# Forgetting attention in a hybrid decoder layer: the low part of exp made against PSUM, and the row sums split between GpSimd and a column of ones

## The chip, the cores and the metric

The kernel runs on one core of one Trainium2 chip. The metric is the device time of one execution in microseconds (us), lower is better. The engines are TensorE (PE, and PEld for its weight loads), VectorE (DVE), ScalarE (ACT), GpSimd (POOL) and SyncE (SP), which here only issues DMAs. All five run their own instruction streams in order and meet at semaphores.

## The reference

One decoder layer: an RMS norm, one input projection of 2048 x 1024 activations to 5656 columns, three mixers side by side, one output projection, and the residual. All in float32. The mixers are forgetting attention (8 heads of 64), a Mamba-2 scan and a gated linear recurrence. The change touches attention only:

```python
def fox_attention(q, k, v, log_f, q_g, k_g):      # cut
    q = rms_norm(q, q_g); k = rms_norm(k, k_g)
    c = jnp.cumsum(log_f, axis=1)
    # per block of 128 queries, per head:
    logits = einsum(q_i, kt) * scale + (c_i[..., :, None] - ck[:, :, None, :])
    logits = where(kpos <= qpos, logits, -inf)
    p = softmax(logits)
    return einsum(p, vt)
```

## The kernel before

**Two parts of a number.** TensorE's fast float32 form (float32r) rounds its operands. So the kernel splits a float32 tile into a rounded part, called h (high), and the rest, called l (low), and multiplies the parts: h by h, h by l, l by h. A split is usually a copy on ACT into a float32r tile and a subtraction on DVE.

**Stages.** The projections come first (until about 1262 us), and write q, k (high and low), v (`v_d`, per head 128 columns: 64 of each part) and the gate to DRAM. Then comes attention, with pieces of the output projection (the "filler") woven in, until about 2027 us. The rest of the output projection ends the kernel.

**Units and blocks.** A unit is one head and one block of 256 queries (`sb` from 0 to 7); there are 64, most heads in rising order of `sb`. For a unit, the keys are taken 256 at a time. One such step, here called a block and in the code a pair `(j, kp)`, is the element of the schedule; there are 288. The last block of a unit (`kp == sb`) lies on the diagonal and has 384 columns instead of 512.

For one block the steps are these:

- `score(j, kp)`: four matmuls (L974, L975) into a PSUM tile `T` (pool `psT`, three buffers), keys on the partitions, queries in the columns. On the diagonal one more adds the mask (L979). ACT makes e = exp(-T) into an SBUF tile (L982, pool `a4`, four buffers), copies it to `ph`, rounded (L985, pool `a5`, five buffers), and DVE makes `pl = e - ph` (L986). GpSimd adds e to the unit's running sum `acc` (L993, L996). At the unit's last block GpSimd folds that to `w` (L1000, L1001, L1004), ACT rounds it to `ah` (L1007), and GpSimd subtracts for `al` (L1008).
- `av(j, kp)`: four matmuls into the unit's PSUM tile `O` (two buffers), left half: v (128 columns, 64 high, 64 low) by `ph` (L1024) and by `pl` (L1026). Rows 0 to 63 of `O` gather high v, rows 64 to 127 low v.
- `finish(j)`: two matmuls of a matrix of ones `onr` with `ah` and `al` put the row sums of the softmax into the right half of `O` (L1034, L1035). ACT copies the lower half of `O` (L1039), DVE adds the upper half (L1040), GpSimd multiplies by the gate (L1041). The result and the sums go to DRAM (L1044, L1046); the division comes later, in the output projection.

**Maxima.** Before a unit's scores the row maxima are needed. `maxima(j)` makes them from its own matmuls (L932, PSUM tile `S`, two buffers) and DVE reductions (L937, L940, L942), in steps spread over the blocks of the unit before. Its first step also issues loads on SP: q for the next pair of units (`load_q`, L804 and two more), the gate, and once per head the next head's k and v (`load_head`). `flip(j)` turns the maxima into a row: a transpose on PE (L956) and two copies on ACT (L957, L958) into row 96 of the tile `q3`, which the score matmuls read. There are two `q3` buffers, one for each pair of units.

**Order.** A loop over the blocks calls, in turn, `score` of block i, the flip and the maxima steps that fall on i, `av` of block i - 3 (`AVL = 3`), `finish` of a unit whose last `av` was one block before, and a share of filler. The tile framework's scheduler then orders each engine's stream by a timing model of its own, with the program's order as the priority, and it adds the semaphores and gives out buffers.

Of the kernel before, what the change touches and what calls it, by code (L numbers as in the profile page):

```python
# [8 lines left out]
F32 = mybir.dt.float32  # L9
F32R = mybir.dt.float32r  # L10
# [8 lines left out]
P = 128  # L19
# [17 lines left out]
HP = 700  # L37
AHEAD = 1
AVL = 3
NDV = 3  # L40
UP, DOWN = (0, 1, 2, 3, 4, 5, 6, 7), (7, 6, 5, 4, 3, 2, 1, 0)
ORD = (DOWN,) + (UP,) * 6 + (DOWN,)
# [5 lines left out]
def hybrid_block(ctx, tc, x, norm_g, w_in, q_norm_g, k_norm_g, forget_b, ssd_conv_w, ssd_conv_b,  # L48
# [314 lines left out]
    def group_v(vpool, g):  # L363
        cols = [(C_V + g * 256, 256)]
        if g == 0:
            cols += [(C_F, 8), (C_DT, 16)]
        w = weights(cols)
        for t2 in range(8):
            if g == 0:
                pss = [proj_tok(w, t2 * 2 + i, f"pv{g}_{t2 * 2 + i}") for i in range(2)]  # L370
            else:
                ps = proj_tok2(w, t2, f"pv{g}_{t2}")
                pss = [ps[:, i, :] for i in range(2)]
            for i, ps in enumerate(pss):
                t = t2 * 2 + i
                vs = vpool.tile([P, 4, P], F32R, name=f"vs{g}_{t}", tag="qk")
                pv = ps[:, 0:256].rearrange("p (h d) -> p h d", d=64)
                A.activation(vs[:, :, 0:64], pv, AF.Copy, scale=0.5)
                V.scalar_tensor_tensor(vs[:, :, 64:128], pv, 0.5, vs[:, :, 0:64].bitcast(F32),
                                       op0=ALU.mult, op1=ALU.subtract)  # L380
                if g == 0:
                    V.tensor_copy(etot[:, t, 0:8], ps[:, 256:264])
                    V.tensor_copy(dt[:, t, :], ps[:, 264:280])
                dma(v_d[t * P:(t + 1) * P, g * 4:g * 4 + 4, :], vs.bitcast(F32))
# [345 lines left out]
    for c in range(NT):  # L730
        for g in range(2):
            nxt = ssd_unit(c, g)
            if store is not None:
# [11 lines left out]
    cx = ExitStack()  # L745
    kc = cx.enter_context(tpool(name="kc", bufs=1, side="right"))
    kvA = cx.enter_context(tpool(name="kvA", bufs=1, side="right"))
    kq = cx.enter_context(tpool(name="kq", bufs=2, side="right"))
    units = [(h, sb) for h in range(8) for sb in ORD[h]]

    zm = kc.tile([P, 640], F32, name="zm")
    G.memset(zm, 0.0)
    G.affine_select(out=zm[:, 512:640], in_=zm[:, 512:640], pattern=[[-1, P]],
                    compare_op=ALU.is_ge, fill=-NEG, base=0, channel_multiplier=1)
    onr = kc.tile([P, P], F32R, name="onr")
    V.tensor_copy(onr, ones)
    idr = kc.tile([P, P], F32R, name="idr")
    V.tensor_copy(idr, ident)
    zmt = kc.tile([P, P], F32R, name="zmt")
# [1 line left out]
    mzs = [kc.tile([P, P], F32, name=f"mz{i}") for i in range(2)]  # L761


    q3s = [kc.tile([P, 512], F32R, name=f"q3{i}") for i in range(2)]
    for i in range(2):
        G.memset(mzs[i], 0.0)
    for q3 in q3s:
        G.memset(q3[64:128, :].bitcast(F32), 0.0)
        G.memset(q3[64:66, :].bitcast(F32), 1.0)
    k2s = {}  # L770

    def make_k2(b):
# [9 lines left out]
    def load_head(h):  # L782
        p, b = divmod(h, 2)
        hs = slice(b * 64, b * 64 + 64)
        pool = kvB if b else kvA
        k2 = k2s[b]
        kx = pool.tile([P, S], F32R, name=f"kx{h}", tag="kx")
        vv = pool.tile([P, NT, P], F32R, name=f"vv{h}", tag="vv")
        dma(k2[0:64, :].bitcast(F32), qk_d["k", "h", p][hs, :])
        dma(k2[64:66, :].bitcast(F32), c_d[h].rearrange("i t l -> i (t l)"))  # L790
        dma(kx[0:64, :].bitcast(F32), qk_d["k", "l", p][hs, :])
        dma(kx[64:128, :].bitcast(F32), qk_d["k", "h", p][hs, :])
        dma(vv.bitcast(F32), v_d[:, h, :].rearrange("(t p) c -> p t c", p=P))
        heads[h] = k2, kx, vv

    def load_q(j):
        h, sb = units[j]
        p, b = divmod(h, 2)
        hs = slice(b * 64, b * 64 + 64)
        q3 = q3s[j // 2 % 2]  # L800
        qx = kq.tile([P, 512], F32R, name=f"qx{j}", tag="qx")
        sb -= sb % 2
        qs = slice(sb * 256, sb * 256 + 512)
        dma(q3[0:64, :].bitcast(F32), qk_d["q", "h", p][hs, qs])  # L804
        dma(qx[0:64, :].bitcast(F32), qk_d["q", "h", p][hs, qs])
        dma(qx[64:128, :].bitcast(F32), qk_d["q", "l", p][hs, qs])
        qs_[j // 2] = q3, qx
# [91 lines left out]
    psO = pcx.enter_context(tpool(name="psO", bufs=PB[2], space=PSUM))  # L899
    psP = pcx.enter_context(tpool(name="psP", bufs=PB[3], space=PSUM))  # L900
    make_k2(1)
    U = [{} for _ in units]

    def maxima(j):
# [55 lines left out]
    def score(j, kp):  # L960

        h, sb = units[j]
        u = U[j]
        k2, kx, vv = heads[h]
        q3, qx = qs_[j // 2]
        o = (sb % 2) * 256
        last = kp == sb
        n = 384 if last else 512
        pt = psT.tile([P, 512], F32, name=f"T{j}_{kp}", tag="T")
        for jj in range(2):  # L970
            ks = slice((kp * 2 + jj) * P, (kp * 2 + jj + 1) * P)
            qs = slice(o + P if last and jj else o, o + 256)
            ps = pt[:, 256 * jj:256 * jj + qs.stop - qs.start]
            T.matmul(ps, k2[:, ks], q3[:, qs], start=(jj == 0), stop=False, skip_group_check=True)  # L974
            ins = T.matmul(ps, kx[:, ks], qx[:, qs], start=False, stop=True, skip_group_check=True)  # L975
        if last:

            pv = pt.rearrange("p (a b) -> p a b", b=256)[:, :, 0:P]
            ins = T.matmul(pv, idr, zmt.unsqueeze(1).broadcast_to([P, 2, P]), start=False,  # L979
                           stop=True, skip_group_check=True)  # L980
        e = a4.tile([P, 512], F32, name=f"e{j}_{kp}", tag="e")
        A.activation(e[:, 0:n], pt[:, 0:n], AF.Exp, scale=-1.0)  # L982
        ph = a5.tile([P, 512], F32R, name=f"ph{j}_{kp}", tag="ph")
        pl = a5.tile([P, 512], F32R, name=f"pl{j}_{kp}", tag="pl")
        A.copy(ph[:, 0:n], e[:, 0:n])  # L985
        V.tensor_tensor(pl[:, 0:n], e[:, 0:n], ph[:, 0:n].bitcast(F32), op=ALU.subtract)  # L986
        u[kp] = ph, pl
        if not last:
            if kp == 0:
                u["acc"] = e  # L990
            elif kp == 1:
                acc = a2.tile([P, 512], F32, name=f"ac{j}", tag="ac")
                G.tensor_tensor(acc, u["acc"], e, op=ALU.add)  # L993
                u["acc"] = acc
            else:
                G.tensor_tensor(u["acc"], u["acc"], e, op=ALU.add)  # L996
            return ins
        if sb > 0:
            w = a2.tile([P, 256], F32, name=f"w{j}", tag="w")
            G.tensor_tensor(w, u["acc"][:, 0:256], u["acc"][:, 256:512], op=ALU.add)  # L1000
            G.tensor_tensor(w, w, e[:, 0:256], op=ALU.add)  # L1001
        else:
            w = e
        G.tensor_tensor(w[:, P:256], w[:, P:256], e[:, 256:384], op=ALU.add)  # L1004
        u["ah"] = a2.tile([P, 256], F32R, name=f"ah{j}", tag="ah")
        u["al"] = a2.tile([P, 256], F32R, name=f"al{j}", tag="al")
        A.copy(u["ah"], w[:, 0:256])  # L1007
        G.tensor_tensor(u["al"], w[:, 0:256], u["ah"].bitcast(F32), op=ALU.subtract)  # L1008
        return ins

    def av(j, kp):

        h, sb = units[j]
        u = U[j]
        vv = heads[h][2]
        if kp == 0:
            u["O"] = psO.tile([P, 512], F32, name=f"O{j}", tag="O")
        po = u["O"]
        ph, pl = u.pop(kp)
        for jj in range(2):  # L1020
            kt = kp * 2 + jj
            qs = slice(P if kp == sb and jj else 0, 256)
            cs = slice(256 * jj, 256 * jj + 256 - qs.start)
            T.matmul(po[:, qs], vv[:, kt, :], ph[:, cs], start=(kt == 0), stop=False,  # L1024
                     skip_group_check=True)
            T.matmul(po[:, qs], vv[:, kt, :], pl[:, cs], start=False, stop=(kt == 2 * sb + 1),  # L1026
                     skip_group_check=True)

    def finish(j):
# [1 line left out]
        h, sb = units[j]  # L1031
        u = U[j]
        po = u["O"]
        T.matmul(po[:, 256:512], onr, u["ah"], start=False, stop=False, skip_group_check=True)  # L1034
        T.matmul(po[:, 256:512], onr, u["al"], start=False, stop=True, skip_group_check=True)  # L1035

        tm = a2.tile([64, 512], F32, name=f"tm{j}", tag="tm")
        to = a2.tile([64, 256], F32, name=f"to{j}", tag="to")
        A.copy(tm, po[64:128, :])  # L1039
        V.tensor_tensor(to, po[0:64, 0:256], tm[:, 0:256], op=ALU.add)  # L1040
        G.tensor_tensor(to, to, u["za"], op=ALU.mult)  # L1041
        p, b = divmod(h, 2)
        cs = slice(sb * 256, (sb + 1) * 256)
        dma(at_d[p][b * 64:b * 64 + 64, cs], to)  # L1044
        qt = slice(sb * 2, sb * 2 + 2)
        dma(s_d[qt, h:h + 1, :].rearrange("i o t -> o i t"),  # L1046
            tm[0:1, 256:512].rearrange("o (i t) -> o i t", i=2))
        if h == 7:

            sr = a2.tile([16, P], F32, name=f"sr{j}", tag="sr")  # L1050
# [117 lines left out]
    begin = [tasks.index((j, 0)) for j in range(len(units))]  # L1168
    at = {}
    for j in range(1, len(units)):  # L1170
        a, b = max(0, begin[j - 1] - 1), begin[j] - 1
        st = maxima(j)
        for i, f in enumerate(st):
            at.setdefault(a + i * (b - a) // len(st), []).append(f)
# [52 lines left out]
```

## Time and profile before

| | us |
|---|---|
| median of 3 runs | 2217.47 (2216.0 to 2223.02) |
| the profiled execution | 2201.74 |
| its span, first to last instruction | 2200.0 |
| attention, first score matmul to last `av` | 1262 to 2027 |

| engine | busy over the span, us | share |
|---|---|---|
| PE | 2048.2 | 93% |
| DVE | 1433.3 | 65% |
| ACT | 1019.2 | 46% |
| POOL | 880.2 | 40% |

How to read the rows: a group's row has line, engine, operation, out<-in, shapes and count, then busy us and mean ns of one, then the engine's idle time just before such instructions and what ended it. A row of one line alone has min/median/max in ns and first and last start. A row of waits has the total in us, the number and the longest. A matmul's record covers its passage through the array, so records of neighbouring matmuls overlap and a busy PE is not PE at its peak. The granted clock (PEclk) is TensorE's clock as a share of full speed.

### The profile page before, as it was taken

What the parts mean: (1) busy time and instruction counts of PE and PEld (TensorE: products, weight loads), DVE (VectorE), ACT (ScalarE), POOL (GpSimd) and SP (SyncE); (2) the same over time, 40 slices, a digit from 0 to 9 for tenths busy, and PEclk for the clock granted to TensorE, in tenths of its full rate; (3) what the DMA queues carried; (4) which work ended last, traced back from release to release, by engine and by line L of the source; (5) the groups of instructions that cost most, each with busy time, mean ns of one, the idle gap of its engine ahead of it and who ended that gap; (6) DMA issues with size and microseconds to landing.
All of it is one profiled execution on the core that took longest, in us unless ns stands there. A gap on an engine that the chain in (4) does not pass through costs nothing. (4 is left out here: it accounts for less than half of the span.)

```text
span 2200.0 us, 34666 instructions
## 1 busy us (share of the span) xinstructions
PE 2048.2 (93%) x11941; PEld 1762.5 (80%) x11941; DVE 1433.3 (65%) x2513; ACT 1019.2 (46%) x2113; POOL 880.2 (40%) x898
## 2 busy tenths in 40 slices
PE   7999999999999998999999988888888888988999
PEld 6898888899898987878889777777777776767887
DVE  6657555736456466767654576877787776887333
ACT  7534454525345345444433446555565555554110
POOL 0100000413223145456520167766777776766110
PEclk9999999999999999999999999988999999997999
DMA  5322232121121456677662555252535435232454
GB/s 175 101 76 60 71 104 87 38 61 60 39 74 50 119 161 195 180 213 207 176 185 80 182 146 136 92 137 70 151 109 140 126 93 130 73 111 83 152 169 139
DMA packets 260466, 261.30 MB, mean 119 GB/s; under 512 B 26773, under 2 KB 198833, under 8 KB 258737
## 3 DMA queue, kind: packets, MB, share of 16 engines
q1 hardware_dynamic: 260128, 259.05, 40.3%
q8 instruction: 94, 1.54, 0.3%
q0 software_dynamic: 160, 0.03, 0.1%
q14 instruction: 84, 0.68, 0.1%
HBM read 164.22 MB, written 94.77 MB: 118 GB/s over the span
## 5 line engine op out<-in xcount | busy, mean ns | idle before, releaser
L986 DVE TENSOR_TENSOR pl<-e,ph 128x512 fp32r<-128x512 f32 (+1 forms) x288 | 338.2, 1197 | 46.4 <-ACT ph L985 46.2
L1095 PE MATMUL po<-woh,mh 128*128 128x512 f32 x512 | 208.5, 407 | 5.7 <-DVE xr L1103 3.1
L1026 PE MATMUL O<-pl,vv 128*128 128x256 f32 x576 | 162.9, 313 | 48.8 <-DVE pl L986 47.9
L1096 PE MATMUL po<-wol,mh 128*128 128x512 f32 x512 | 205.6, 401 | 0.0
L1097 PE MATMUL po<-woh,ml 128*128 128x512 f32 x512 | 205.4, 401 | 0.0
L982 ACT ACTIVATE e<-T 128x512 f32<-128x512 f32 (+1 forms) x288 | 162.8, 575 | 85.5 <-PE T L975 48.4
L996 POOL TENSOR_TENSOR ac<-ac,e 128x512 f32<-128x512 f32 x120 | 185.9, 1549 | 23.2 <-ACT e L982 16.1
L1026 PEld LDWEIGHTS O<-pl,vv 128*128 128x128 f32 x576 | 114.8, 199 | 76.3 <-DVE pl L986 73.2
L974 PE MATMUL T<-q,k 128*128 128x256 f32 x576 | 163.2, 305 | 12.9 <-ACT q L958 12.5
L1024 PE MATMUL O<-ph,vv 128*128 128x256 f32 x576 | 154.1, 286 | 15.2 <-ACT ph L985 5.6
L942 DVE TENSOR_REDUCE mc<-S 128x1 f32<-128x512 f32 x192 | 129.9, 682 | 57.8 <-PE S L932 57.6
L985 ACT CAST ph<-e 128x512 fp32r<-128x512 f32 (+1 forms) x288 | 165.3, 597 | 2.8 <-PE O L1024 0.6
L1083 POOL TENSOR_TENSOR ml<-mt,mh 128x512 fp32r<-128x512 f32 x48 | 67.1, 1399 | 244.1 <-ACT mh L1082 244.0
L975 PE MATMUL T<-qx,kx 128*128 128x256 f32 x576 | 156.6, 299 | 0.0
L356 PE MATMUL pxx<-uh,wh 128*128 128x512 f32 x384 | 152.8, 400 | 1.8 <-ACT uh L301 1.7
L357 PE MATMUL pxx<-ul,wh 128*128 128x512 f32 x384 | 153.1, 400 | 0.0
L358 PE MATMUL pxx<-uh,wl 128*128 128x512 f32 x384 | 150.9, 395 | 0.0
L340 PE MATMUL pqk<-wh,uh 128*128 128x256 f32 x512 | 149.4, 292 | 0.0
L344 PE MATMUL pqk<-wh,ul 128*128 128x256 f32 x512 | 149.3, 292 | 0.0
L342 PE MATMUL pqk<-wl,uh 128*128 128x256 f32 x512 | 148.8, 291 | 0.0
L412 DVE SCALAR_TENSOR_TENSOR accx<-rtx,cv,accx 128x512 f32<-128x512 f32 x144 | 108.0, 752 | 57.8 <-ACT accx L409 54.8
L342 PE MATMUL pzs<-wl,uh 128*128 128x256 f32 x512 | 143.5, 281 | 0.0
(351 smaller groups left out, 5925.4 us busy)
## 6 DMA issues: line engine op xcount, KB each, us to landing
ab<-acs_d SPq DMA_DIRECT2D x64, 256.0 KB
pt_d<-xr SPq DMA_DIRECT2D x64, 256.0 KB
wr<-in_w_in_dram SPq DMA_DIRECT2D x112, 128.0 KB
xt<-in_x_dram SPq DMA_DIRECT2D x16, 512.0 KB
xs_d<-stx SPq DMA_DIRECT2D x32, 256.0 KB
v_d<-vs SPq DMA_DIRECT2D x32, 256.0 KB
wr<-in_w_in_dram SPq DMA_DIRECT2D x128, 64.0 KB
zs_d<-zs SPq DMA_DIRECT2D x32, 256.0 KB
```

Of the source, the lines that this page charges most:

```text
L342: T.matmul(ps[:, i, :], h[k][:, sl], wl[k], start=False, stop=False, skip_group_check=True)
L974: T.matmul(ps, k2[:, ks], q3[:, qs], start=(jj == 0), stop=False, skip_group_check=True)
L975: ins = T.matmul(ps, kx[:, ks], qx[:, qs], start=False, stop=True, skip_group_check=True)
L982: A.activation(e[:, 0:n], pt[:, 0:n], AF.Exp, scale=-1.0)
L985: A.copy(ph[:, 0:n], e[:, 0:n])
L986: V.tensor_tensor(pl[:, 0:n], e[:, 0:n], ph[:, 0:n].bitcast(F32), op=ALU.subtract)
L996: G.tensor_tensor(u["acc"], u["acc"], e, op=ALU.add)
L1024: T.matmul(po[:, qs], vv[:, kt, :], ph[:, cs], start=(kt == 0), stop=False, skip_group_check=True)
L1026: T.matmul(po[:, qs], vv[:, kt, :], pl[:, cs], start=False, stop=(kt == 2 * sb + 1), skip_group_check=True)
L1095: T.matmul(ps, mh[:, j, :], h, start=(j == 0), stop=False)
L1096: T.matmul(ps, mh[:, j, :], l, start=False, stop=False)
L1097: T.matmul(ps, ml[:, j, :], h, start=False, stop=(j == 3))
```

## The change

- `score`: no tile e. ACT makes exp(-T) twice, into `ph` (rounded, SBUF) and back into `T` (full, PSUM). DVE makes `pl = T - ph`, one source in PSUM. GpSimd adds `ph` only.
- The order of v's parts is swapped in DRAM (low in 0 to 63, high in 64 to 127), and the SBUF tile `vv` gets two more columns, set to one by GpSimd once per head.
- `av`: the matmul with `pl` takes 65 columns of `vv` (high v and the ones) and adds into the right half of `O`: rows 0 to 63 get high v by `pl`, row 64 the sums of `pl`. The product of low v and `pl` is no longer made.
- `finish`: `onr` has 65 columns, of which only the last is ones, so the sums of `ph` land on row 64 too. ACT makes two copies instead of one, DVE two additions instead of one, with three buffers each.
- Schedule: with `LT = 2` the steps of `maxima` (with their loads) come one block earlier, the flip stays; a third pair of q tiles (`q3`, `qx`), and `qx` moves from a pool of its own to them.

```diff
+LT = 2
...
-                A.activation(vs[:, :, 0:64], pv, AF.Copy, scale=0.5)
-                V.scalar_tensor_tensor(vs[:, :, 64:128], pv, 0.5, vs[:, :, 0:64].bitcast(F32),
+                A.activation(vs[:, :, 64:128], pv, AF.Copy, scale=0.5)
+                V.scalar_tensor_tensor(vs[:, :, 0:64], pv, 0.5, vs[:, :, 64:128].bitcast(F32),
                                        op0=ALU.mult, op1=ALU.subtract)
...
-    onr = kc.tile([P, P], F32R, name="onr")
-    V.tensor_copy(onr, ones)
+    onr = kc.tile([P, 65], F32R, name="onr")
+    G.memset(onr[:, 0:64].bitcast(F32), 0.0)
+    G.memset(onr[:, 64:65].bitcast(F32), 1.0)
...
+    def make_q(pool):
+        i = len(q3s)
+        q3 = pool.tile([P, 512], F32R, name=f"q3{i}")
+        G.memset(q3[64:128, :].bitcast(F32), 0.0)
+        G.memset(q3[64:66, :].bitcast(F32), 1.0)
+        q3s.append(q3)
+        qxs.append(pool.tile([P, 512], F32R, name=f"qx{i}"))
...
-        vv = pool.tile([P, NT, P], F32R, name=f"vv{h}", tag="vv")
+        vv = pool.tile([P, NT, 130], F32R, name=f"vv{h}", tag="vv")
...
-        dma(vv.bitcast(F32), v_d[:, h, :].rearrange("(t p) c -> p t c", p=P))
+        dma(vv[:, :, 0:128].bitcast(F32), v_d[:, h, :].rearrange("(t p) c -> p t c", p=P))
+        G.memset(vv[:, :, 128:130].bitcast(F32), 1.0)
...
-        q3 = q3s[j // 2 % 2]
-        qx = kq.tile([P, 512], F32R, name=f"qx{j}", tag="qx")
+        q3, qx = q3s[j // 2 % 3], qxs[j // 2 % 3]
...
-        e = a4.tile([P, 512], F32, name=f"e{j}_{kp}", tag="e")
-        A.activation(e[:, 0:n], pt[:, 0:n], AF.Exp, scale=-1.0)
         ph = a5.tile([P, 512], F32R, name=f"ph{j}_{kp}", tag="ph")
         pl = a5.tile([P, 512], F32R, name=f"pl{j}_{kp}", tag="pl")
-        A.copy(ph[:, 0:n], e[:, 0:n])
-        V.tensor_tensor(pl[:, 0:n], e[:, 0:n], ph[:, 0:n].bitcast(F32), op=ALU.subtract)
+        A.activation(ph[:, 0:n], pt[:, 0:n], AF.Exp, scale=-1.0)
+        A.activation(pt[:, 0:n], pt[:, 0:n], AF.Exp, scale=-1.0)
+        V.tensor_tensor(pl[:, 0:n], pt[:, 0:n], ph[:, 0:n].bitcast(F32), op=ALU.subtract)
         u[kp] = ph, pl
+        e = ph.bitcast(F32)
...
         else:
-            w = e
+            G.tensor_copy(w, e[:, 0:256])
...
-            T.matmul(po[:, qs], vv[:, kt, :], ph[:, cs], start=(kt == 0), stop=False,
-                     skip_group_check=True)
-            T.matmul(po[:, qs], vv[:, kt, :], pl[:, cs], start=False, stop=(kt == 2 * sb + 1),
+            q2 = slice(256 + qs.start, 512)
+            T.matmul(po[:, qs], vv[:, kt, 0:128], ph[:, cs], start=(kt == 0),
+                     stop=(kt == 2 * sb + 1), skip_group_check=True)
+            T.matmul(po[0:65, q2], vv[:, kt, 64:129], pl[:, cs], start=False, stop=False,
                      skip_group_check=True)
...
-        tm = a2.tile([64, 512], F32, name=f"tm{j}", tag="tm")
-        to = a2.tile([64, 256], F32, name=f"to{j}", tag="to")
-        A.copy(tm, po[64:128, :])
-        V.tensor_tensor(to, po[0:64, 0:256], tm[:, 0:256], op=ALU.add)
+        to = a3.tile([64, 256], F32, name=f"to{j}", tag="to")
+        su = a3.tile([1, 256], F32, name=f"su{j}", tag="su")
+        A.copy(to, po[64:128, 0:256])
+        A.copy(su, po[64:65, 256:512])
+        V.tensor_tensor(to, po[0:64, 0:256], to, op=ALU.add)
+        V.tensor_tensor(to, po[0:64, 256:512], to, op=ALU.add)
...
-        a, b = max(0, begin[j - 1] - 1), begin[j] - 1
+        a, b = max(0, begin[j - 1] - LT), begin[j] - LT
```

More of the change, by code (lines that the diff above doesn't have):

```diff
@@ L747, in hybrid_block @@
     kvA = cx.enter_context(tpool(name="kvA", bufs=1, side="right"))
-    kq = cx.enter_context(tpool(name="kq", bufs=2, side="right"))
     units = [(h, sb) for h in range(8) for sb in ORD[h]]
@@ L761, in hybrid_block @@
     mzs = [kc.tile([P, P], F32, name=f"mz{i}") for i in range(2)]
-    q3s = [kc.tile([P, 512], F32R, name=f"q3{i}") for i in range(2)]
+    q3s, qxs = [], []
+    def make_q(pool):
[5 more added lines that the diff above has]
+        qxs.append(pool.tile([P, 512], F32R, name=f"qx{i}"))
     for i in range(2):
         G.memset(mzs[i], 0.0)
-    for q3 in q3s:
-        G.memset(q3[64:128, :].bitcast(F32), 0.0)
-        G.memset(q3[64:66, :].bitcast(F32), 1.0)
+    for i in range(2):
+        make_q(kc)
     k2s = {}
@@ L901, in hybrid_block @@
     make_k2(1)
+    make_q(a1)
     U = [{} for _ in units]
@@ L997, in score @@
             return ins
+        w = a2.tile([P, 256], F32, name=f"w{j}", tag="w")
         if sb > 0:
-            w = a2.tile([P, 256], F32, name=f"w{j}", tag="w")
             G.tensor_tensor(w, u["acc"][:, 0:256], u["acc"][:, 256:512], op=ALU.add)
@@ L1006, in score @@
         u["al"] = a2.tile([P, 256], F32R, name=f"al{j}", tag="al")
-        A.copy(u["ah"], w[:, 0:256])
-        G.tensor_tensor(u["al"], w[:, 0:256], u["ah"].bitcast(F32), op=ALU.subtract)
+        A.copy(u["ah"], w)
+        G.tensor_tensor(u["al"], w, u["ah"].bitcast(F32), op=ALU.subtract)
         return ins
@@ L1033, in finish @@
         po = u["O"]
-        T.matmul(po[:, 256:512], onr, u["ah"], start=False, stop=False, skip_group_check=True)
-        T.matmul(po[:, 256:512], onr, u["al"], start=False, stop=True, skip_group_check=True)
-        tm = a2.tile([64, 512], F32, name=f"tm{j}", tag="tm")
-        to = a2.tile([64, 256], F32, name=f"to{j}", tag="to")
-        A.copy(tm, po[64:128, :])
-        V.tensor_tensor(to, po[0:64, 0:256], tm[:, 0:256], op=ALU.add)
+        T.matmul(po[0:65, 256:512], onr, u["ah"], start=False, stop=False, skip_group_check=True)
+        T.matmul(po[0:65, 256:512], onr, u["al"], start=False, stop=True, skip_group_check=True)
+        to = a3.tile([64, 256], F32, name=f"to{j}", tag="to")
[4 more added lines that the diff above has]
+        V.tensor_tensor(to, po[0:64, 256:512], to, op=ALU.add)
         G.tensor_tensor(to, to, u["za"], op=ALU.mult)
@@ L1046, in finish @@
         dma(s_d[qt, h:h + 1, :].rearrange("i o t -> o i t"),
-            tm[0:1, 256:512].rearrange("o (i t) -> o i t", i=2))
+            su.rearrange("o (i t) -> o i t", i=2))
         if h == 7:
```

## The prediction

> **What bounds the kernel now.** I read the first lines of the page, then the busy time by window. The attention stage runs from its first score matmul at 1262 us to its last at 2027 us; what follows is output projection alone.
>
> ```profile
> PE 2048.2 (93%) x11941; PEld 1762.5 (80%) x11941; DVE 1433.3 (65%) x2513; ACT 1019.2 (46%) x2113; POOL 880.2 (40%) x898
> ```
>
> ```profile
> core 0: us, PE busy (x) PEld busy (x) DVE busy (x) ACT busy (x) POOL busy (x), PEclk, DMA share, GB/s
> 1262.00:2027.00 765.00, 657.36 (x3671) 554.76 (x3670) 604.36 (x1043) 424.85 (x880) 540.56 (x503) 0.93 0.41 115
> 2027.00:2200.00 173.00, 167.47 (x725) 137.86 (x724) 67.69 (x153) 18.47 (x31) 19.28 (x17) 0.97 0.48 148
> ```
>
> In 765 us, DVE is busy 79%, POOL 71%, ACT 56%. PE's 86% is not its work: the timeline (start, duration) shows how far its records overlap, the groups how many there are.
>
> ```profile
> 1709.23 0.41 PE L975 MATMUL T<-qx,kx 128*128 128x256 f32 x1
> 1709.44 0.41 PE L974 MATMUL T<-q,k 128*128 128x256 f32 x1
> 1711.04 0.39 PE L1096 MATMUL po<-wol,mh 128*128 128x512 f32 x1
> 1711.27 0.39 PE L1097 MATMUL po<-woh,ml 128*128 128x512 f32 x1
> 1711.73 0.28 PE L974 MATMUL T<-q,k 128*128 128x256 f32 x1
> 1711.85 0.28 PE L975 MATMUL T<-qx,kx 128*128 128x256 f32 x1
> ```
>
> ```profile
> L932 PE MATMUL S<-k,q 96*128 96x512 f32 (+3 forms) x311 | 127.2, 415 | 6.0 <-DVE mc L942 2.9 <-DMA q<-qh_d 2.1 <-DVE mz L937 0.2
> L1095 PE MATMUL po<-woh,mh 128*128 128x512 f32 x268 | 111.2, 415 | 4.8 <-DVE xr L1103 3.1 <-DVE xr L1101 0.8
> ```
>
> Starts lie 0.12 us apart for 256 columns and 0.23 for 512 at full clock, 0.21 for 256 at the throttled clock 2 us before. At full clock the stage's matmuls (288 blocks of eight and some 250 at the units' ends with up to 256 columns; 3 x 268 and 311 with up to 512) need 2554 x 0.12 + 1115 x 0.23 = 563 us. So about 200 of the 765 us are waits and slow clock. The next view, waits of PE's weight loads (the loads stand first in line), names them: us in total, times, longest.
>
> ```profile
> PEld O L1026 <- DVE pl L986: 73.2, 99, 3.1
> PEld T L974 <- ACT q L958: 23.7, 35, 1.9
> PEld pm L956 <- DVE mz L940: 14.2, 20, 1.8
> PEld O L1034 <- ACT ah L1007: 10.3, 14, 2.2
> PEld S L932 <- DVE mc L942: 7.8, 18, 1.3
> PEld O L1024 <- DVE to L1040: 5.4, 3, 3.5
> PEld O L1024 <- DVE mz L940: 5.3, 2, 2.6
> PEld O L1035 <- POOL al L1008: 4.5, 11, 1.4
> ```
>
> Most of it ends with DVE, half of that with the subtraction pl = e - ph. The groups of DVE by shape, and two lines outside the busy part of POOL, say why (last rows: min/median/max).
>
> ```profile
> L986 DVE TENSOR_TENSOR pl<-e,ph 128x512 fp32r<-128x512 f32 x224 | 286.5, 1299 | 45.3 <-ACT ph L985 45.1
> L986 DVE TENSOR_TENSOR pl<-e,ph 128x384 fp32r<-128x384 f32 x64 | 53.6, 842 | 1.1 <-ACT ph L985 1.1
> L937 DVE CUSTOM_DVE_ANT_0 jk<-S,zm 128x384 f32<-128x384 f32 x31 | 17.0, 548 | 8.5 <-PE S L932 8.5
> L1040 DVE TENSOR_TENSOR to<-O,tm 64x256 f32<-64x256 f32 x62 | 25.3, 410 | 14.5 <-ACT tm L1039 7.2 <-DMA at_d<-to 6.8
> L1101 DVE SCALAR_TENSOR_TENSOR xr<-po,rsn,xr 128x256 f32<-128x256 f32 x64 | 28.1, 471 | 11.3 <-PE po L1097 11.3
> L1101 DVE SCALAR_TENSOR_TENSOR xo<-po,rsn,xo 128x256 f32<-128x256 f32 x52 | 21.7, 474 | 18.3 <-DMA xo<-pt_d 15.5 <-PE po L1097 2.8
> L1075 DVE TENSOR_TENSOR ml<-mt,mh x16: 683/685/1133, 2018.6 to 2185.3; 128x512 fp32r<-128x512 f32 x16
> L398 DVE SCALAR_TENSOR_TENSOR zt<-th,pza x8: 676/684/689, 1211.4 to 1250.9; 128x512 f32<-128x512 f32 x8
> ```
>
> The same subtraction of two SBUF tiles takes 685 ns (L1075) where POOL is nearly idle, 1299 ns in attention. L1101 reads PSUM and one SBUF tile: 471 ns in attention, 474 mostly in the tail, so POOL does not stretch it. The stretch belongs to two SBUF sources.
>
> **The change part by part.** *pl from PSUM.* One source moves to PSUM. Nearest rows: 684 ns (L398) for 512 columns and 548 (L937) for 384. DVE gives back 224 x (1299 - 684) + 64 x (842 - 548) = 157 us. Ends: 0 if the stretch stays, 157 if it goes; L1101 is nearest in form, so 157. [...]
>
> What does PE get of it? Its 99 waits on pl average 0.74 us; each pl comes 0.6 us sooner, and so do those queued before it, but a faster PE asks sooner. I take three quarters of 73.2: 55 us. Of the 18.5 us behind mc, to and mz, which share DVE's queue, I take half: 9.
>
> *POOL.* The other party gets free too. Means against the shortest:
>
> ```profile
> L996 POOL TENSOR_TENSOR ac<-ac,e x120: 1254/1619/2727, 1265.0 to 2003.7; 128x512 f32<-128x512 f32 x120
> L1001 POOL TENSOR_TENSOR w<-w,e x56: 721/987/1667, 1276.6 to 2020.4; 128x256 f32<-128x256 f32 x56
> L996 POOL TENSOR_TENSOR ac<-ac,e 128x512 f32<-128x512 f32 x120 | 185.9, 1549 | 23.2 <-ACT e L982 16.1 <-PE po L1097 1.2
> L1001 POOL TENSOR_TENSOR w<-w,e 128x256 f32<-128x256 f32 x56 | 53.3, 952 | 3.7 <-ACT e L982 0.2
> L775 POOL MEMSET k<- 1x2048 f32 x1 | 1.8, 1799 | 0.1
> ```
>
> 120 x (1549 - 1254) + 56 x (952 - 721) = 48 us off POOL in these two groups. It adds ph in place of e, at the same time as before. The one path to PE is the end of a unit (ah, al: 14.8 us of waits); a third goes: 5. New on POOL: eight copies for one-block units (at 952 ns, 8 us) and one memset per head behind vv's release. The memset's price is at most L775's 1.8 us; what stands behind it on POOL are the adds of the next units, which PE needs four blocks later. Ends: 0, and 7 heads x 3 blocks x 2.66 us = 56 us of a standing POOL; I put in 1 us a head, 7 lost, since POOL catches up in those four blocks.
>
> *ACT.* The copy to ph becomes the second exponential, PSUM to PSUM.
>
> ```profile
> L985 ACT CAST ph<-e 128x512 fp32r<-128x512 f32 x224 | 134.2, 621 | 1.5 <-PE O L1024 0.4
> L982 ACT ACTIVATE e<-T 128x512 f32<-128x512 f32 x224 | 132.0, 599 | 64.0 <-PE T L975 48.4 <-DVE pl L986 6.3 <-DVE mc L937 1.7
> L1039 ACT COPY tm<-O 64x512 f32<-64x512 f32 x63 | 36.5, 583 | 39.8 <-PE O L1035 21.0 <-DMA s_d<-tm 16.0 <-DVE pl L986 1.8
> ```
>
> 288 x (599 - 621) = -6 us; no row writes PSUM from ACT: it could be dearer or cheaper, and I take 599, the same function from the same tile. In finish, tm's 583 becomes two copies, each of half the columns or fewer and so under 583: between 0 and +37 us. Together at most 31 us on 425, hidden by ACT's 44% idle; without that cover ACT would be at 456 of 663. DVE's second add in finish costs 64 x 410 = 26 us, so DVE's net is 604 - 157 + 26 = 473. The three result buffers in place of two free ACT's 16.0 us behind s_d; nothing of that reaches PE.
>
> *Thinner second matmul, swapped halves of v.* Same count, same 256 columns.
>
> ```profile
> L1026 PEld LDWEIGHTS O<-pl,vv x576: 186/188/338, 1267.7 to 2026.9; 128*128 128x128 f32 x192
> L956 PEld LDWEIGHTS pm<-ident,mz x64: 160/163/284, 1260.5 to 2020.1; 128*97 128x97 f32 x64
> ```
>
> Fewer weight columns load sooner (163 against 188), but matmuls start every 0.12 us, so the loads already overlap. Ends 0 and 576 x 25 ns = 14 us; I take 0. The other vv and vs edits move the same bytes.
>
> *Maxima one block earlier (LT = 2), third q buffer.* A block takes 765 / 288 = 2.66 us. PE's waits for mz and then for q (14.2 + 23.7 = 38) are at most 1.9 us long. One block more of lead covers them, unless the flip's own copies behind two exponentials hold: I take four fifths, 30. The moved steps issue their q, za and head loads on SP one block earlier; the third buffer keeps the q loads from waiting for readers there. I put nothing in for it: little of PE's waiting ends with a DMA.
>
> *Clock.* Granted 0.93 in the stage, 0.97 after it. Fewer gaps should give about 0.95: 0.02 x 563, some 10 us. [...]
>
> *T held longer.* T was free after the first exponential; now after both and pl. Three buffers at 2.66 us allow a stay of 8.0; scores, exponentials and pl need 0.5 + 0.6 + 0.6 + 0.7 = 2.4, and 5.6 remain for DVE's queue. I charge nothing here; it is the main rival.
>
> Sum: 55 + 9 + 5 + 30 + 10 - 7 = 102 us. Attention then takes 663 us, with DVE at 71%, POOL (541 - 48 + 8) at 76%, ACT at most 69%: below DVE's 79% of now. The profiled execution took 2201.7, so 2100 against it; the median is 15.8 above it, hence **2115**.
>
> **The rivals.** *T takes back half.* PE loses its lead: scores of block i+3 wait for pl of block i, where only its second half of av waited. For it: bursts such as this one of DVE are what the lead absorbs; against: three pl shrink from 3.84 to 2.05 us.
>
> ```profile
> 1699.82 3.84 DVE L986 TENSOR_TENSOR pl<-e,ph 128x512 fp32r<-128x512 f32 x3
> ```
>
>  Half of 102 gone: 2166.
>
> *Slower: the T loop decides.* If every block waits for T as long as pl's waiters do now, 288 x 0.74 = 213 us replace 73; less the other 47 of the sum, +93: 2310. It decides from a mean wait of (73 + 47) / 288 = 0.42 us per block. Against: it needs the 5.6 us to be used up regularly.
>
> *Nothing moves.* PE's waits for pl pass to POOL, still over 70% loaded, at each unit's end: 2217.
>
> *DVE was the pace.* Every us off DVE counts, 131, plus LT's 30: 2056. For it: DVE is the fullest engine; against: it idles 161 us.
>
> **How the numbers follow.** Forecast (2065 to 2150) 0.52; half taken back 0.22; nothing 0.06; slower 0.12; below 2065, 0.08. A change within 0.3% (6.7 us) can't be told from none. Faster 0.82, same 0.06, slower 0.12. The range 2060 to 2222 leaves out the slower case and most of the last: 0.19.
>
> **What would show it.** pl at 512 columns near 690 ns (above 900: the stretch was not POOL's doing); the second exponential near 600; DVE's total 1433 down by 130; L996's mean under 1400; waits for pm and q under 10 us; scores waiting for pl under 30 us. If those exceed 120 us, or POOL's memset holds its queue for several us a head, the prediction is wrong.

## The result, and the profile after

The changed kernel takes 2067.61 us (median of 4, 2064.18 to 2072.21) against 2216.73 before: a ratio of 0.9329, interval 0.9294 to 0.9365, or 149 us less. The forecast of faster held, and the time lies in the range (2065 to 2150), 2.6 us from its fast end; the point, 2115, gave 102 of the 149 us. The profiled execution of the kernel before was some 15 us faster than its median, so the profiles show 136.5 us of the difference.

The first lines of the page and the busy time by window, with the attention stage now from 1260 to 1892 us:

```profile
PE 1970.9 (96%) x11941; PEld 1713.8 (83%) x11941; DVE 1303.0 (63%) x2576; ACT 1007.7 (49%) x2177; POOL 803.1 (39%) x918
```

```profile
core 0: us, PE busy (x) PEld busy (x) DVE busy (x) ACT busy (x) POOL busy (x), PEclk, DMA share, GB/s
1260.00:1892.00 632.00, 582.20 (x3674) 506.53 (x3672) 473.63 (x1106) 413.94 (x945) 464.23 (x517) 0.98 0.49 139
1892.00:2063.00 171.00, 165.62 (x725) 136.40 (x723) 70.72 (x157) 18.48 (x31) 19.19 (x17) 0.99 0.49 152
```

Attention shrank from 765 to 632 us, so 133 of the 136.5 us between the two spans (2200.0 and 2063.5) come from there; the projections before it and the tail behind it became about 2 us shorter each. DVE is down from 604 to 474 us, POOL from 541 to 464, ACT from 425 to 414. PE does as many matmuls as before, at a granted clock of 0.98 in place of 0.93.

The waits of PE's weight loads in attention (us in total, times, longest):

```profile
PEld pm L969 <- DVE mz L953: 19.0, 21, 4.0
PEld T L987 <- ACT q L971: 14.4, 24, 2.1
PEld S L945 <- ACT q L971: 7.6, 12, 1.0
...
PEld S L945 <- DVE mc L955: 5.5, 8, 1.8
PEld O L1042 <- DVE pl L998: 5.1, 7, 1.2
PEld O L1050 <- ACT ah L1021: 3.7, 7, 1.3
...
PEld O L1051 <- POOL al L1022: 0.9, 2, 0.7
PEld T L987 <- DVE pl L998: 0.6, 1, 0.6
```

The wait for pl is all but gone: 73.2 us before, 5.1 now, and T waits for pl only 0.6 us. The flip's waits are not gone: 14.2 + 23.7 before, 19.0 + 14.4 now, with 7.6 of S beside them. The groups by shape in that window:

```profile
L998 DVE TENSOR_TENSOR pl<-T,ph 128x512 fp32r<-128x512 f32 x224 | 152.7, 685 | 39.9 <-ACT T L997 37.9 <-PE po L1113 0.3 <-PE S L945 0.3
L998 DVE TENSOR_TENSOR pl<-T,ph 128x384 fp32r<-128x384 f32 x64 | 35.2, 551 | 9.0 <-ACT T L997 8.3
...
L1010 POOL TENSOR_TENSOR ac<-ac,ph 128x512 f32<-128x512 f32 x120 | 156.1, 1301 | 23.1 <-ACT ph L996 17.2 <-DMA xr<-pt_d 1.2
L806 POOL MEMSET vv<- 128x32 f32 x6 | 0.8, 132 | 1.4 <-PE O L1042 1.3
...
L997 ACT ACTIVATE T<-T 128x512 f32<-128x512 f32 x224 | 133.6, 596 | 0.0
```

pl takes 685 ns (1299 before) and GpSimd's addition 1301 (1549): both sides of the old conflict got quicker. The second exponential, PSUM to PSUM, takes 596 ns, the first 597.

### The profile page after: what moved, and what is told of

It reads as the page before. It is cut to its first block, busy times and chain, and to the rows that moved or that the text cites. A ratio compares the mean times of both kernels' runs of the same rounds, so it can differ in the third digit from the quotient of the medians.

```text
span 2063.5 us, 35018 instructions
## 1 busy us (share of the span) xinstructions
PE 1970.9 (96%) x11941; PEld 1713.8 (83%) x11941; DVE 1303.0 (63%) x2576; ACT 1007.7 (49%) x2177; POOL 803.1 (39%) x918
## 4 chain that ended last, share of the span: by engine, by line
PE 41%; DMA 6%; DVE 4%; ACT 4%; issue 2%; POOL 2%; SPq 0%; DVEq 0%; POOLq 0%; ACTq 0%
PE po L1112 5%; PE po L1113 5%; PE po L1114 5%; PE T L987 3%; PE T L988 3%; PE S L945 2%; PE O L1040 2%; PE O L1042 2%; PE py L691 2%; PE pza L358 1%; PE pza L359 1%; PE pza L357 1%; DMA ab<-acs_d 1%; PE pqk L341 1%; PE pqk L343 1%
## 5 line engine op out<-in xcount | busy, mean ns | idle before, releaser
L998 DVE TENSOR_TENSOR pl<-T,ph 128x512 fp32r<-128x512 f32 (+1 forms) x288 | 187.3, 655 | 48.8 <-ACT T L997 46.3
L996 ACT ACTIVATE ph<-T 128x512 fp32r<-128x512 f32 (+1 forms) x288 | 165.1, 573 | 88.7 <-PE T L988 60.5
L1010 POOL TENSOR_TENSOR ac<-ac,ph 128x512 f32<-128x512 f32 x120 | 156.1, 1301 | 23.1 <-ACT ph L996 17.2
L997 ACT ACTIVATE T<-T 128x512 f32<-128x512 f32 (+1 forms) x288 | 164.9, 572 | 0.0
L987 PE MATMUL T<-q,k 128*128 128x256 f32 x576 | 150.0, 287 | 9.6 <-ACT q L971 6.8
L1040 PE MATMUL O<-ph,vv 128*128 128x256 f32 x576 | 149.0, 280 | 0.9 <-ACT ph L996 0.4
L1042 PE MATMUL O<-pl,vv 128*65 128x256 f32 x576 | 142.2, 279 | 3.4 <-DVE pl L998 2.8
L988 PE MATMUL T<-qx,kx 128*128 128x256 f32 x576 | 143.7, 283 | 0.0
L345 PE MATMUL pzs<-wh,ul 128*128 128x256 f32 x512 | 143.4, 280 | 0.0
L341 PE MATMUL pzs<-wh,uh 128*128 128x256 f32 x512 | 143.0, 281 | 0.0
```

Of the source, the lines that this page charges most:

```text
L341: T.matmul(ps[:, i, :], h[k][:, sl], wh[k], start=(k == 0 and i == 0), stop=False, skip_group_check=True)
L345: ins = T.matmul(ps[:, i, :], l[k][:, sl], wh[k], start=False, stop=last, skip_group_check=True)
L998: V.tensor_tensor(pl[:, 0:n], pt[:, 0:n], ph[:, 0:n].bitcast(F32), op=ALU.subtract)
L1040: T.matmul(po[:, qs], vv[:, kt, 0:128], ph[:, cs], start=(kt == 0), stop=(kt == 2 * sb + 1), skip_group_check=True)
L1042: T.matmul(po[0:65, q2], vv[:, kt, 64:129], pl[:, cs], start=False, stop=False, skip_group_check=True)
```

## The experiments

Theory P says that the stretch of pl by GpSimd was the cost. Rival L says that the earlier maxima and the third q buffer bring much of the gain. Each kernel was timed in three rounds beside the kernel before; ratios are to that kernel. Its own median moved between 2213.07 and 2216.73 us from one set of rounds to the next, so between kernels of different sets the ratios are the better measure.

**One part alone: pl from PSUM (x3_psum).**

```diff
 # kernel before (cut)
-        A.activation(e[:, 0:n], pt[:, 0:n], AF.Exp, scale=-1.0)
-        A.copy(ph[:, 0:n], e[:, 0:n])
-        V.tensor_tensor(pl[:, 0:n], e[:, 0:n], ph..., op=ALU.subtract)
+        A.activation(ph[:, 0:n], pt[:, 0:n], AF.Exp, scale=-1.0)
+        A.activation(pt[:, 0:n], pt[:, 0:n], AF.Exp, scale=-1.0)
+        V.tensor_tensor(pl[:, 0:n], pt[:, 0:n], ph..., op=ALU.subtract)
+        e = ph.bitcast(F32)
```

> The kernel before with one part of the change: both exponentials and pl from PSUM, GpSimd adding ph, no tile e. LT, the q buffers, v's layout, the second matmul and finish stay as before (so the sums of pl are left out of the row sums). Theory P (the stretch of pl by GpSimd was the cost, and a source in PSUM takes it away): pl at 512 columns falls from 1299 to about 685 ns and this part alone brings at least 110 of the 149 us, so 2065 to 2105 us. Rival L (the earlier maxima and the third q buffer bring much of it): under 75 us, over 2140. Rival T (the longer stay of T eats part of the gain until LT and the rest give it back): between, with scores waiting for pl over 20 us.

Measured: 2113.46 us, ratio 0.9541 (0.9517 to 0.9564), 102 us less than the 2215.71 beside it. That is two thirds of the gain, a little under what theory P asked for. The time lies in the band of rival T, but not by its cause: scores wait 0.5 us in all for pl at T. pl is at 686 ns and PE's wait for it at 9.2 us. But other waits came up. The window, the group of pl, and waits in the window:

```profile
1268.00:1944.00 676.00, 603.34 (x3672) 528.05 (x3672) 458.81 (x1042) 410.67 (x881) 463.68 (x512) 0.95 0.47 130
```

```profile
L985 DVE TENSOR_TENSOR pl<-T,ph 128x512 fp32r<-128x512 f32 x224 | 153.4, 686 | 41.9 <-ACT T L984 40.7 <-PE po L1096 0.3 <-PE po L1097 0.3
```

```profile
ACT tm L1039 <- DMA s_d<-tm: 35.0, 9, 5.7
...
DVE to L1040 <- DMA at_d<-to: 28.3, 6, 6.1
...
PEld pm L956 <- DVE mz L940: 19.7, 22, 3.6
PEld T L974 <- ACT q L958: 19.3, 37, 0.8
...
PEld O L1034 <- ACT ah L1007: 19.0, 18, 4.2
...
PEld O L1026 <- DVE pl L985: 9.2, 12, 2.6
```

DVE lost 146 us of work there, the stage 89. `finish` now waits longer for its result buffers, whose stores stand in SP's queue: tm 35.0 us (16.0 before) and to 28.3 (6.8 before). PE's wait for ah rose from 10.3 to 19.0 us.

**Then the schedule (x9_psum_lt2).** x3_psum with `LT = 2` and the third pair of q tiles, as in the diff of the change.

> The kernel x3_psum plus LT = 2 and the third pair of q tiles; the sums of pl are left out as there. What is then still missing of the change is the column of ones, v's layout, and the new finish. Theory P: within 10 us of x3_psum, since in the changed kernel PE's waits for mz and q stayed at about 41 us (38 before). Rival L: at least 30 us faster than x3_psum.

Measured: 2091.91 us, ratio 0.9443 (0.9423 to 0.9462), 22 us less than x3_psum. It lies between the two expectations. The stage takes 659 us at a clock of 0.96. PE's waits in it:

```profile
PEld T L982 <- ACT q L966: 17.2, 28, 2.8
PEld S L940 <- ACT q L966: 16.1, 8, 5.8
PEld O L1042 <- ACT ah L1015: 10.5, 9, 4.4
PEld pm L964 <- DVE mz L948: 9.8, 19, 0.8
```

The waits for mz and q are 43 us (40 in x3_psum, with S's 0.7), so the 22 us did not come from them; the wait for ah fell from 19.0 to 10.5, that for pl from 9.2 to 4.7.

**Undone: LT = 1 (x2_lt1).**

```diff
 # changed kernel
-LT = 2
+LT = 1
```

> The changed kernel with LT = 1, the third q pair kept. My prediction gave LT 30 us; its waits did not fall, so theory P now expects 0 to 10 us lost: 2065 to 2080, with waits for mz and q near 40 us in both. Rival L: at least 30 us lost, over 2097, and these waits over 70 us.

Measured: 2080.58 us, ratio 0.9386 (0.9357 to 0.9415): 13 us lost, again between the expectations, and its interval just meets the changed kernel's (0.9294 to 0.9365). PE's waits for the flip, 20.3 + 21.3 us and 1.3 of S, come to 43 us, about as much as with LT = 2 (19.0 + 14.4 + 7.6 = 41):

```profile
PEld T L987 <- ACT q L971: 21.3, 38, 1.0
PEld pm L969 <- DVE mz L953: 20.3, 27, 2.3
PEld O L1042 <- DVE pl L998: 10.5, 16, 1.7
```

So the lead is worth some 13 us alone and 22 together with the third pair of q tiles, but hardly by these waits; the wait for pl (10.5 us against 5.1) and the clock (0.96 against 0.98) are worse too.

**Undone: the result buffers (y5_two).**

```diff
 # changed kernel
-        to = a3.tile([64, 256], F32, name=f"to{j}", tag="to")
-        su = a3.tile([1, 256], F32, name=f"su{j}", tag="su")
+        to = a2.tile([64, 256], F32, name=f"to{j}", tag="to")
+        su = a2.tile([1, 256], F32, name=f"su{j}", tag="su")
```

> The changed kernel with two result buffers (to, su) in finish in place of three. It tells whether the 24 us between x9_psum_lt2 and the changed kernel come from these buffers, and whether their loss in x1_sbuf counted there. If they do: 10 to 25 us slower, 2078 to 2093. If not (the 24 us come from the thinner weights and the scheduler's other order): within 8 us, 2060 to 2076.

Measured: 2092.62 us, ratio 0.9463 (0.9440 to 0.9486): 25 us lost by the medians, 30 by the ratios, all that lies between x9_psum_lt2 and the changed kernel. Waits in attention:

```profile
ACT to L1054 <- DMA at_d<-to: 41.9, 9, 9.2
DVE to L1056 <- ACT su L1055: 35.0, 10, 7.6
...
PEld S L945 <- ACT q L971: 26.2, 11, 7.7
...
PEld O L1050 <- ACT ah L1021: 14.3, 10, 4.9
```

and the same wait with three buffers, in the changed kernel:

```profile
ACT to L1054 <- DMA at_d<-to: 7.6, 5, 3.7
```

ACT's copy out of O stands up to 9.2 us for a buffer whose store has not gone out. Behind it in ACT's queue are the copies of the flip and ah, and PE waits for those: S for q 26.2 us against 7.6, ah 14.3 against 3.7. The longest of these waits, in y5_two's timeline (start, duration, and in brackets the idle time before it):

```profile
1446.23 0.37 ACT L1054 COPY to<-O 64x256 f32<-64x256 f32 x1 [9.24 <-DMA at_d<-to]
...
1447.16 0.26 ACT L971 CAST q<-pm 1x128 fp32r<-1x128 f32 x1
1447.44 0.41 ACT L1021 CAST ah<-w 128x256 fp32r<-128x256 f32 x1
```

```profile
1447.47 0.29 PEld L945 LDWEIGHTS S<-k,q 96*128 96x128 f32 x1 [7.72 <-ACT q L971]
```

PE stood 7.7 of ACT's 9.2 us. With three buffers the chain is short.

**Undone: the source of pl (x1_sbuf).** The changed kernel with the second exponential in SBUF again.

```diff
 # changed kernel (cut); a4 with 3 buffers; to and su with 2
-        A.activation(pt[:, 0:n], pt[:, 0:n], AF.Exp, scale=-1.0)
-        V.tensor_tensor(pl[:, 0:n], pt[:, 0:n], ph..., op=ALU.subtract)
+        e2 = a4.tile([P, 512], F32, name=f"e{j}_{kp}", tag="e")
+        A.activation(e2[:, 0:n], pt[:, 0:n], AF.Exp, scale=-1.0)
+        V.tensor_tensor(pl[:, 0:n], e2[:, 0:n], ph..., op=ALU.subtract)
```

> The changed kernel, but the second exponential goes to an SBUF tile again (three buffers, for room; to and su get two), so pl has two SBUF sources and T is free before pl. Theory P: pl at 512 columns is back at 1200 to 1300 ns, PE's weight loads wait over 50 us for it, the granted clock in attention falls to about 0.93, and at least 100 of the 149 us are lost: 2165 to 2225. Rival S (what counts is the other order and the shorter sums, the source of pl does not): under 50 us lost, below 2120.

Measured: 2177.20 us, ratio 0.9825 (0.9802 to 0.9848), 110 us lost. Since it also has two result buffers, the fair comparison is y5_two, so the source of pl costs 85 us of it (80 by the ratios). The tile e2 has three buffers where e had four; ACT waited 2.7 us in all for one. Window, group and wait:

```profile
1264.00:2002.00 738.00, 632.59 (x3671) 537.93 (x3671) 603.31 (x1104) 410.29 (x941) 544.18 (x515) 0.92 0.43 119
```

```profile
L999 DVE TENSOR_TENSOR pl<-e,ph 128x512 fp32r<-128x512 f32 x224 | 267.3, 1201 | 33.7 <-ACT e L998 32.9
```

```profile
PEld O L1043 <- DVE pl L999: 52.8, 65, 2.7
```

pl is back at 1201 ns, PE waits 52.8 us for it, the clock is back at 0.92, and POOL too is back at 544 us. T is free early there, and it does not help.

**Is it GpSimd that stretches pl? (x4_noadds).** The kernel before without the running sum, which its row sums then lack.

```diff
 # kernel before (cut)
-                acc = a2.tile([P, 512], F32, name=f"ac{j}", tag="ac")
-                G.tensor_tensor(acc, u["acc"], e, op=ALU.add)
-                u["acc"] = acc
+                u["acc"] = e
             else:
-                G.tensor_tensor(u["acc"], u["acc"], e, op=ALU.add)
+                u["acc"] = e
```

> The kernel before without GpSimd's running sum (the 168 additions of e to acc, some 248 us of GpSimd in attention); the row sums are then of the last blocks only, with 1 added ahead of the reciprocal. pl keeps its two SBUF sources. Theory P: pl at 512 columns falls from 1299 to under 900 ns though nothing of pl changed, and the kernel comes to 2070 to 2130. Rival: the stretch is pl's own (its reads of e and ph): it stays above 1200 ns, and the time above 2190.

Measured: 2136.14 us, ratio 0.9647 (0.9627 to 0.9667), just slower than the band of theory P and far from the rival's. Window, groups and PE's wait for pl:

```profile
1263.00:1960.00 697.00, 618.77 (x3672) 538.57 (x3672) 487.51 (x1048) 423.94 (x881) 285.77 (x335) 0.94 0.45 127
```

```profile
L986 DVE TENSOR_TENSOR pl<-e,ph 128x512 fp32r<-128x512 f32 x224 | 172.9, 784 | 56.1 <-ACT ph L985 55.8
L986 DVE TENSOR_TENSOR pl<-e,ph 128x384 fp32r<-128x384 f32 x64 | 47.0, 734 | 13.2 <-ACT ph L985 13.0
```

```profile
PEld O L1024 <- DVE pl L986: 21.3, 34, 1.8
```

The same instruction on the same two SBUF tiles falls from 1299 to 784 ns when POOL's work falls from 541 to 286 us, and PE's wait for it from 73.2 to 21.3 us. That settles whose doing the stretch was. One source in PSUM goes further: 685 ns with POOL at 464 us in the changed kernel, 686 with POOL at 464 in x3_psum. How pl and the additions hold each other up no run here shows; in the kernel before the longest pl took 3.70 us, in x4_noadds 1.68.

**The longer stay of T (x5_before_t2, x6_after_t2).**

```diff
 # each kernel
-PB = (2, 3, 2, 1)
+PB = (2, 2, 2, 1)
```

> The kernel before with two buffers for T in place of three. There T is free after the first exponential, about 1.7 us after its first matmul. Both theories: 0 to 30 us slower than before.

> The changed kernel with two buffers for T in place of three. T's stay there is 3.3 us from first score matmul to the end of pl, and a block takes 632 / 288 = 2.2 us, so two buffers allow 4.4. If the longer stay is near its limit (the rival of my prediction), at least 60 us slower, over 2127; if three buffers leave it clear room, 10 to 50 us slower, 2078 to 2118.

Measured: 2210.34 us, ratio 0.9977 (0.9963 to 0.9991), and 2065.29 us, 0.9325 (0.9308 to 0.9342). Neither lost anything; both expectations of a loss in the changed kernel were wrong. With two buffers PE waits for pl at T 6.2 us in all; the flip's waits are in the same view:

```profile
PEld S L945 <- ACT q L971: 7.6, 8, 3.0
...
PEld T L987 <- DVE pl L998: 6.2, 13, 1.7
...
PEld T L987 <- ACT q L971: 3.8, 11, 0.8
...
PEld pm L969 <- DVE mz L953: 2.7, 3, 1.2
```

So the rival of the T loop is refuted, with a whole PSUM bank to spare.

**More lead, and a use for the bank (x8_lt3, y1_lt3_s3, y4_lt3_p2, y3_lt3_s3_rate).** x8_lt3 has `LT = 3`, a third tile `mz` and the head's loads at `j % 8 == 3`. The next two add `PB = (3, 2, 2, 1)` and `PB = (2, 2, 2, 2)`. The last has `PB = (3, 2, 2, 1)` and `RATE = 275`.

> The changed kernel with LT = 3: the maxima one block earlier still (a third tile for the maxima, the next head's loads one unit later, so that nothing in use is overwritten). LT = 1 cost 13 us. If the lead of the maxima is what the flip lacks, another 5 to 15 us faster, 2052 to 2063, with waits for mz under 8 us; if the flip waits for DVE's queue and for its two copies on ACT whatever the lead, 2060 to 2075 with waits for mz and q at 30 us or more.

> x8_lt3 with a PSUM bank moved from T (two buffers, which cost nothing in x6_after_t2) to S (three). PE's largest remaining waits there are S for the copies of the flip, whose tile pm has a buffer of S (14.2 us), and for mc and mz: a third buffer should take 10 to 20 us, 2041 to 2051. If the order that the scheduler makes matters more than the buffers, 2055 to 2070.

> x8_lt3 with T's third bank given to the output projection's tile (two buffers), so that its next matmuls need not wait for DVE's additions to xr. These waits and the unexplained ones before it are 8 to 15 us: 2046 to 2056 if they go, 2058 to 2065 if the filler's place in the order hides them.

> y1_lt3_s3 with RATE = 275: 15 more steps of filler (three matmuls each, 10 us in the dense tail) inside attention, where PE still waits some 70 us. If they fall into waits, 5 to 10 us faster than y1_lt3_s3; if they lengthen attention by as much, the same within 4 us.

| kernel | median us | ratio to before | interval |
|---|---|---|---|
| changed kernel | 2067.61 | 0.9329 | 0.9294 to 0.9365 |
| x8_lt3 | 2061.19 | 0.9302 | 0.9284 to 0.9319 |
| y1_lt3_s3 | 2056.45 | 0.9290 | 0.9268 to 0.9311 |
| y4_lt3_p2 | 2062.25 | 0.9313 | 0.9288 to 0.9338 |
| y3_lt3_s3_rate | 2049.98 | 0.9270 | 0.9244 to 0.9297 |

Each interval overlaps its neighbour's, so the single steps are not shown. The median of x8_lt3 lies in both of its bands; y1_lt3_s3 and y4_lt3_p2 miss the gain that was hoped for and lie in their second bands; y3_lt3_s3_rate is 6.5 us under y1_lt3_s3, in its first. This last is the fastest kernel run, 18 us under the changed kernel by the medians and 13 by the ratios, at the edge of what the intervals tell apart (0.9297 and 0.9294). In x8_lt3 PE's wait of pm for mz is down to 1.0 us, while S and T still wait for q:

```profile
PEld S L947 <- ACT q L973: 14.2, 20, 4.7
...
PEld T L989 <- ACT q L973: 7.6, 17, 1.2
```

In y1_lt3_s3 the first of these fell to 4.1 us, but the wait of T for pl rose from 2.6 to 12.4: in these profiles, what the bank gave to S it took from T.

## Why the prediction was right, and where its sum was off

Done one after the other, three parts add up to the gain: pl from PSUM 102 us (x3_psum), the lead with its q tiles 22 (x9_psum_lt2), the third result buffer 24 to 25. The column of ones, the thinner matmul and the new `finish` moved nothing that shows: with two buffers (y5_two) they stand at x9_psum_lt2's time. Taken out of the changed kernel, the source of pl is worth 80 to 85 us and the lead alone some 13. That the time lies in the range is in part luck: its fast end is 2.6 us away, and one of the four runs (2064.18) is beyond it. Against the terms:

- **pl from PSUM.** The mechanism and the durations were right: 685 and 551 ns against 684 and 548; DVE's total down by 130.3 us against 130 or 131 worked out; POOL's mean addition 1301 against "under 1400". POOL gave back more than was worked out, 76 us in attention against 40, since its other additions were stretched too (w<-ac 1058 ns before, 749 after). Of PE's waits, that for pl fell by 68 us, where 55 were taken; those behind mc, to and the mz that held O by 13 (9 taken); those for ah and al by 10 (5 taken). Only the first came with this part: in x3_psum the wait for pl fell by 64 us, but ah and al rose from 14.8 to 21.7, and mc, to and mz came to 16 against 18.5. The three terms charged 69 us to this part, which measured 102 with its share of the clock.
- **The waits as a whole.** The waits of PE's weight loads in attention add up to 164 us before, 103 in x3_psum and 77 in the changed kernel. So 88 us went, and the sum without the clock's 10 had 92. That these agree is luck: pl, DVE's queue, ah and al gave 91 where 69 were taken, and the flip 5 where 30 were. The other 45 of the stage's 133 us lie outside these waits.
- **The clock.** This was the term most under-sized: 0.95 expected, 0.98 granted, so by the term's own rule 0.05 x 563 = 28 us, not 10. The record of the clock in the traces has two values, 1.00 and 0.50; in attention before, 0.50 comes in stretches of 3.4, 6.8, 10.2 and, at the stage's end, 13.7 us. As an estimate from the means, 2 x 0.07 x 765 = 107 us stood at 0.50 before and 2 x 0.02 x 632 = 25 after; half of the difference, 41 us, is the most that this can have brought. One such stretch stands behind short waits. These rows are the time before it and the stretch itself (the matmuls at 0.21 us in the prediction are from it), and what PE waited for in the first of the two:

```profile
1700.63:1704.04 3.41, 1.81 (x11) 1.40 (x11) 3.41 (x4) 0.04 (x1) 3.10 (x4) 1.00 0.23 68
1704.04:1710.87 6.83, 6.12 (x23) 4.77 (x22) 3.80 (x9) 2.82 (x7) 1.54 (x3) 0.50 0.04 9
```

```profile
PE O L1026 <- DVE pl L986: 1.6, 3, 0.9
```

PE was busy for 1.81 of 3.41 us, with three waits for pl (1.6 us in all), and the clock stood at 0.50 for the 6.83 us behind them. In the whole stage before, no matmul waited longer than 3.1 us. That gaps lower the clock was the author's estimate; no run shows what lowers it. Across the kernels the clock is by and large higher where the stage is shorter (stage length and clock: 765 us, 0.93; 738, 0.92; 697, 0.94; 676, 0.95; 632, 0.98; but 629, 0.96 in x6_after_t2). No run moved the clock alone, so its share of the gain is not measured.
- **LT = 2: 30 us taken, 13 to 22 measured.** The step that failed is "One block more of lead covers them": the waits for mz and q stayed at 33 us, where under 10 was to show it. The lead does not decide over them alone: with the same LT they are, with S's wait for q, 41 us in the changed kernel, 14 in x6_after_t2 and 52 in y5_two, which differ in buffers and in the order that the scheduler made. How the lead brings its 13 to 22 us stays open; the rows show shorter waits for ah and pl, and no run has the third q pair alone.
- **Result buffers: "nothing of that reaches PE".** This was wrong, and worth 24 to 25 us by the medians. The 16.0 us of ACT were read from the kernel before, in which ACT had slack. In a faster one the wait grew to 35.0 (x3_psum) and 41.9 (y5_two), and PE got it through ACT's queue, as y5_two's timeline shows.
- **T held longer and the memset.** Charged nothing and 7. T's stay costs nothing even with two buffers; the memset takes 132 ns and waited 1.3 us in all.
- **ACT.** 596 ns against 599 taken, inside the bounds.

Of the rivals, "DVE was the pace" came nearest in number (2056), but not in mechanism: x3_psum took 146 us off DVE for 102 us of time, and the other 47 us came from the schedule and the buffers. x1_sbuf has as much DVE work in attention as the kernel before (603 and 604 us) and is 39 us faster. The rival of T was refuted by x6_after_t2.

## What to carry to other kernels

Compare the duration of an instruction in a busy stage with the same form in a quiet one: here 1299 ns in attention against 685 (L1075). With two SBUF sources for pl and GpSimd busy for 541 of 765 us, a source in PSUM gave that difference back: pl came to 685 ns and GpSimd's addition went from 1549 to 1301, and holding the PSUM tile longer cost nothing (0.9325 with two buffers of T against 0.9329 with three). A wait of an off-path engine for a store is not free because it is short now: ask what stands behind it in that engine's queue once the big wait is gone, and give the result another buffer (16.0 us of ACT's waits before, 35.0 in x3_psum and 41.9 in y5_two; the third buffer was worth 24 to 25). Where short waits are frequent, look at the granted clock of the time behind them too (0.50 behind the three waits above).

## What was not expected of the hardware

Taking one PSUM bank from T cost nothing (0.9325 against 0.9329), though T is held from the first score matmul to the end of pl. A load of 65 weight columns takes 135 ns in the median where 128 take 188; the matmuls still start 0.12 us apart (rows of the changed kernel: the weight load, then two starts in a row):

```profile
L1042 PEld LDWEIGHTS O<-pl,vv x576: 133/135/231, 1266.1 to 1891.9; 128*65 128x65 f32 x192
```

```profile
1707.51 0.28 PE L1042 MATMUL O<-pl,vv 128*65 128x256 f32 x1
1707.63 0.28 PE L1040 MATMUL O<-ph,vv 128*128 128x256 f32 x1
```

ACT writes PSUM as fast as SBUF here: 596 and 597 ns.
